# Expert weights in tiles of 16 KB a partition, one-product scatter, tokens gathered from the residual, one softmax

## The chip, the cores and the metric

The kernel runs on one core of a Trainium2 chip. The metric is the device time of one execution in microseconds (us). The profile shows TensorE (PE, with its weight loads as PEld), VectorE (DVE), ScalarE (ACT), GpSimd (POOL) and SyncE (SP), which issues most DMAs. Each engine takes its instructions in order.

## The reference, cut to what matters

One layer over 512 tokens of 1024 features: two token mixers (neighbourhood attention, a bidirectional state-space scan), merged by gates and an output projection, and then experts that each choose 64 tokens:

```
x = x + ga1 * rmsnorm(merge(...) @ w_out, n_post_mix)
h = rmsnorm(x, n_pre_ffn) * (1 + sc2) + sh2
aff = softmax(h @ w_router)                   # 512 x 16
gate, idx = top_k(aff.T, 64)                  # 16 experts, 64 tokens each
xg = h[idx]                                   # 16 x 64 x 1024
hid = silu(xg @ w_eg) * (xg @ w_eu)           # 1024 -> 2048
yo = (hid @ w_ed) * gate                      # 2048 -> 1024
out = x + ga2 * rmsnorm(zeros.at[idx].add(yo), n_post_ffn)
```

All is float32. The weights of an expert are three matrices of 8.39 MB; the sixteen experts have 402.7 MB, read once.

## The kernel before

The mixers come first: an input projection in pieces of split float32 products, the scan, attention, the gates and the merge of the branches, all led by PE. The merge writes the merged branch `uh2` and `ul2` (a high and a low part, 8 x 128 features by 512 tokens).

The tokens are held in two orders. The grid has 8 rows of 64 columns, and most of the program has the tokens as h, r, c (8 column groups, 8 rows, 8 columns in a group); `perm_hrc` and `split_hrc` turn one into the other. Before the change the merged branch, the residual `x1` and all that follows keep h, r, c, so `x` is loaded and the output written in pieces of 64 partitions, 8 x 8 rows of the tensor.

The out projection (`out_part`, L1009 to L1021) makes 128 tokens by 256 columns from 24 products, two such pieces in one call for the last half. It needs `g1`, a gain row spread over all partitions, and evacuates into `h2` through one of three PSUM buffers. `post(i)` finishes a tile of 128 tokens: the residual, eight transposes, the router's logits, the softmax and its transpose into `affn`. `scaled(i)` makes the experts' input `h2` from `x1`: a POOL product with `a2`, an ACT copy with the norm's factor, a POOL sum with `s2`. Both rows are spread over the partitions by DMAs on POOL's queue. The program mixes these pieces by hand, `post(i - 1)` and `scaled(i - 2)` after `out_part(i)`.

Top-k takes eight rounds of `max` and `match_replace` on 16 partitions. From the mask come the slots (`slot`), and from them for each pair of experts a one-hot `oh`. `gather` multiplies it with `h2` on PE and copies into `xg`; the first expert's gather is cut up between its first products.

The experts' loop reads its weights in tiles of 1 MB, 8 KB in each partition, from a ring of 15 (`W_RING`), with four more tiles the first time (`W_FIRST`, the 0 tiles). `wtile` hands them out; the letter is the pool. Pool b lies where the out projection's operands lie, the 0 tiles where the routing's tiles lie, so their loads wait for those. Gate and up tiles have rows of 8 KB of DRAM, down tiles two rows of 4 KB for each partition. Each expert: the products for gate and up (`pu`), four transposes of the one-hot times affinity (`pg` to `pgT`), SwiGLU, transposes of `hid`, the down products (`pd`), a copy `yo`, and the scatter: eight products by `pgT`, K = 64, each added into `ya` by DVE. The last expert's down matrix is read in two column halves, rows of 1 KB, so that the closing norm's squares start before the end.

SP's queue has the weight loads in program order, and a load whose tile is not free holds all behind it.

## Time and profile before

| | |
|---|---|
| median of 3 runs | 2150.54 us (2147.04 to 2150.69) |
| profiled execution | 2140.64 us, span 2138.8 us |
| PE busy | 1956.6 us, 91% of the span |
| DVE, ACT, POOL busy | 877.0, 617.4, 315.4 us |
| DMA | 549.42 MB, mean 257 GB/s |
| granted TensorE clock | 0.981 |

The span runs from the first to the last instruction; the execution's own time lies 1.84 us above it. Busy shares are means over stages: about the first half is token mixing, the second the experts. [...] Times within the span start at its first instruction.

### The profile page before, as it was taken

How to read it: one execution, taken by the hardware profiler on the slowest of the kernel's cores; microseconds unless marked ns; L12 is line 12 of the kernel's file. 1: busy time of each engine (PE TensorE's matmuls, PEld its weight loads, DVE VectorE, ACT ScalarE, POOL GpSimd, SP SyncE). 2: the span in 40 equal slices, each digit the busy share in tenths (PEclk: the TensorE clock that was granted, in tenths of full speed). 3: DMA queues.
4: the chain of work that ended last, by engine and by line, in shares of the span. 5: the costliest groups of instructions: out<-in, count | busy, mean ns of one | idle time of the engine just before them, and what ended most of it. 6: DMA issues, size and time to landing. Idle time of an engine off the chain costs nothing.

```text
span 2138.8 us, 26149 instructions
## 1 busy us (share of the span) xinstructions
PE 1956.6 (91%) x10331; PEld 1194.0 (56%) x10331; DVE 877.0 (41%) x1590; ACT 617.4 (29%) x1222; POOL 315.4 (15%) x397
## 2 busy tenths in 40 slices
PE   5999999999999999999985999998989989898985
PEld 3778787776777777788884343342423333242322
DVE  6797777747665657833336011101111111011112
ACT  2466556435555544632222110000000000000001
POOL 3042312243333323200013000000000000000001
PEclk8999999999999999999996999999999999999998
DMA  9344334352332335553485899999999999999996
GB/s 245 89 137 136 92 116 133 104 155 92 111 128 86 118 118 160 166 167 104 158 246 209 336 417 416 416 417 417 418 418 418 416 417 416 416 416 418 418 416 200
DMA packets 190810, 549.42 MB, mean 257 GB/s; under 512 B 14328, under 2 KB 108584, under 8 KB 155872
## 3 DMA queue, kind: packets, MB, share of 16 engines
q1 hardware_dynamic: 174648, 490.90, 60.1%
q0 software_dynamic: 15680, 55.81, 8.1%
q8 instruction: 81, 1.33, 0.3%
q10 hardware_dynamic: 360, 1.05, 0.1%
q14 instruction: 41, 0.34, 0.0%
HBM read 530.76 MB, written 16.94 MB: 256 GB/s over the span
## 4 chain that ended last, share of the span: by engine, by line
PE 50%; DMA 26%; DVE 6%; issue 4%; POOL 3%; ACT 2%; SPq 0%; POOLq 0%; DVEq 0%; ACTq 0%
PE pu L1169 12%; DMA wb<-in_w_exp_down 5%; DMA wb<-in_w_exp_up 5%; PE ps_mm L213 4%; PE ps_mm L219 4%; PE ps_mm L214 4%; DMA wa<-in_w_exp_down 3%; PE px L1136 3%; DMA wc<-in_w_exp_up 3%; PE pd L1209 2%; PE px L1218 2%; PE ps_mm L929 2%; PE ps_mm L928 2%; DMA wc<-in_w_exp_down 2%; PE ps_mm L927 2%
## 5 line engine op out<-in xcount | busy, mean ns | idle before, releaser
L213 PE MATMUL ps_mm<-hh,wh 128*128 128x512 f32 (+1 forms) x648 | 264.3, 408 | 7.1 <-DVE sz L914 4.6
L214 PE MATMUL ps_mm<-hl,wh 128*128 128x512 f32 (+1 forms) x648 | 259.7, 401 | 2.6 <-DVE hl L352 2.6
L219 PE MATMUL ps_mm<-hh,wl 128*128 128x512 f32 (+1 forms) x648 | 260.4, 402 | 0.0
L167 DVE TENSOR_TENSOR wl<-raw,wh 128x1024 fp32r<-128x1024 f32 (+2 forms) x109 | 141.8, 1301 | 195.0 <-ACT wh L166 189.9
L1169 PE MATMUL pu<-wb,xg 128*64 128x512 f32 x792 | 179.7, 596 | 9.5 <-DMA wb<-in_w_exp_up 5.7
L1224 DVE TENSOR_TENSOR ya<-ya,px 128x512 f32<-128x512 f32 x112 | 70.7, 683 | 281.1 <-PE px L1218 280.6
L166 ACT CAST wh<-raw 128x1024 fp32r<-128x1024 f32 (+2 forms) x109 | 117.0, 1074 | 183.3 <-PE ps_mm L928 84.8
L213 PEld LDWEIGHTS ps_mm<-hh,wh 128*128 128x128 f32 (+1 forms) x648 | 122.3, 189 | 41.5 <-issue 14.3
L214 PEld LDWEIGHTS ps_mm<-hl,wh 128*128 128x128 f32 (+1 forms) x648 | 122.5, 189 | 20.8 <-DVE hl L352 3.3
L219 PEld LDWEIGHTS ps_mm<-hh,wl 128*128 128x128 f32 (+1 forms) x648 | 122.5, 189 | 15.7 <-issue 0.8
L1189 DVE SCALAR_TENSOR_TENSOR hid<-hid,pu 128x512 f32<-128x512 f32 x32 | 21.9, 687 | 249.4 <-ACT hid L1188 249.4
L1169 PEld LDWEIGHTS pu<-wb,xg 128*64 128x64 f32 x792 | 54.3, 137 | 124.1 <-issue 97.7
L1154 POOL DMA_DIRECT2D g<-gain_scr x1 | 0.6, 574 | 817.7 <-PE pu L1169 817.7
L1178 DVE TENSOR_TENSOR pg<-oh,aff 128x256 f32<-128x256 f32 x32 | 12.2, 421 | 262.3 <-PE px L1181 223.7
L1209 PE MATMUL pd<-wb,hidT 128*64 128x512 f32 x384 | 89.7, 600 | 16.2 <-DMA wb<-in_w_exp_down 15.8
L480 DVE SCALAR_TENSOR_TENSOR cacc<-pad,cwh,cacc 128x772 f32<-128x772 f32 (+1 forms) x96 | 100.3, 1049 | 9.6 <-ACT cacc L478 8.6
L1169 PE MATMUL pu<-raw,xg 128*64 128x512 f32 x408 | 94.5, 597 | 5.8 <-DMA raw<-in_w_exp_gate 3.0
L1169 PE MATMUL pu<-wc,xg 128*64 128x512 f32 x408 | 95.0, 596 | 4.2 <-DMA wc<-in_w_exp_up 2.5
L1169 PE MATMUL pu<-wa,xg 128*64 128x512 f32 x408 | 94.0, 597 | 4.2 <-DMA wa<-in_w_exp_up 2.5
L1218 PE MATMUL px<-yo,pgT 64*128 64x512 f32 x240 | 82.5, 634 | 9.6 <-ACT yo L1214 9.6
L216 PE MATMUL ps_mm<-ch,wh 128*128 128x256 f32 x280 | 82.0, 293 | 4.3 <-ACT rw L683 4.2
L1188 ACT ACTIVATE hid<-pu 128x512 f32<-128x512 f32 x32 | 19.0, 597 | 221.8 <-PE pu L1169 221.8
(816 smaller groups left out, 3478.6 us busy)
## 6 DMA issues: line engine op xcount, KB each, us to landing
wb<-in_w_exp_up SPq DMA_DIRECT2D x50, 1024.0 KB
wb<-in_w_exp_gate SPq DMA_DIRECT2D x49, 1024.0 KB
wb<-in_w_exp_down SPq DMA_DIRECT2D x48, 1024.0 KB
...
```

The lines of the kernel that those rows point to most:

```text
L166: S.copy(wh, v[:, :, c0:c0 + n])
L167: eng.tensor_tensor(wl, v[:, :, c0:c0 + n], wh.bitcast(F32), op=OP.subtract)
L213: PE.matmul(lat, wh[:, k, :m], hh[:, k, :], start=s, stop=False)
L214: PE.matmul(lat, wh[:, k, :m], hl[:, k, :], start=False, stop=False)
L216: PE.matmul(ctxp, wh[:, k, :m], ch[:, k, :], start=s, stop=False)
L219: PE.matmul(lat, wl[:, k, :m], hh[:, k, :], start=False, stop=e)
L480: E.scalar_tensor_tensor(acc[:, :n], pad[:, j:j + n], w(j), acc[:, :n], op0=OP.mult, op1=OP.add)
L1136: PE.matmul(p[:, k * 128:(k + 1) * 128], h2[:, i, (k0 + k) * 128:(k0 + k + 1) * 128], oh[:, i].rearrange("p e s -> p (e s)"), start=(i == ...
L1169: PE.matmul(acc[q * 2 + b][o * 64:(o + 1) * 64, :], xe[:, k, :], w[:, f:f + 512], start=(k == 0), stop=(k == KT - 1))
L1209: PE.matmul(pd[dh * 64:(dh + 1) * 64, :], l, wd[:, q1 * 1024 + dh * 512:q1 * 1024 + (dh + 1) * 512], start=(n == 0), stop=(n == 15))
L1218: PE.matmul(p, pgT[dh * 64:(dh + 1) * 64, i * 128:(i + 1) * 128], yo[dh * 64:(dh + 1) * 64, :], start=True, stop=True)
L1224: V.tensor_tensor(d, d, p, op=OP.add)
```

## The change

- Weights: every tile has 2 MB, 16 KB in each partition, from one contiguous stretch of DRAM (two neighbouring rows of gate or up, four of down). The ring has eight tiles, ten the first time; pool d lies where the out projection's results lay. The order of the hidden features follows (`hid` is transposed with a stride of four). The last expert's down matrix comes in two halves with rows of 2 KB.
- Tokens: `h2`, `a2`, `s2` and `scaled` are gone. `gather` reads `x1` with a stride of two features, the one-hot is first multiplied by the norm's factor (`ohq`), and scale and shift (`modg`, per feature) are applied where the product is evacuated.
- Softmax: `post` becomes `resid`, `turn`, `logits`, `second`, and one `soft` over the four tiles.
- Scatter: the bare one-hot is transposed (`ohT`, by a product with the identity, both halves of the partitions), the affinity of each slot is a product of one column (`gs`); `yo` is scaled by it and split into a high and a low part that stand in the two halves of the partitions, so that one product with K = 128 adds both.
- Row order: the merged branch is written in the natural order, and `x` and the output move in pieces of 128 partitions.
- `g1` moves from SP's queue to POOL's, ahead of `x`.
- The last expert calls a Sqrt early, on one column.

```diff
-W_RING = "aaacccrrrbbbbbb"
-W_FIRST = "aaacccrrrbbb0000bbb"
+W_RING = "acsrbbbd"
+W_FIRST = "acsrbb00bd"
...
+        modg = rc.tile([128, 16], F32, name="modg")
+        for c0, src, off in ((0, mod_d, 1024), (8, gain_d, 1024)):
+            G.dma_start(modg[:, c0:c0 + 8].rearrange("p (k a) -> p k a", a=2),
+                        bass.AP(tensor=src.tensor, offset=src.offset + off, ap=[[2, 128], [256, 4], [1, 2]]))
+        return wr2, sb, modg
...
-            split_act(uh2[:, j, :], ul2[:, j, :], t1)
+
+            S.copy(perm_hrc(uh2[:, j, :]), split_hrc(t1))
+            V.tensor_tensor(perm_hrc(ul2[:, j, :]), split_hrc(t1), perm_hrc(uh2[:, j, :].bitcast(F32)), op=OP.subtract)
...
-    h2 = ab.tile([128, 4, D], F32, name="h2")
+    qv = ab.tile([128, 4], F32, name="qv")
+    rx, es_rx = pool("rx", side="right")
+    hx = rx.tile([128, 4, D], F32, name="hx")
     rt, es_rt = pool("rt", side="right")
     spD1, es_spD1 = pool("spD1", side="right")
     brow = lambda t, off: bass.AP(tensor=t.tensor, offset=t.offset + off, ap=[[0, 128], [1, D]])
     g1 = rt.tile([128, D], F32, name="g1")
-    a2 = rt.tile([128, D], F32, name="a2")
-    s2 = rt.tile([128, D], F32, name="s2")
-    with tc.high_priority(offset=HP_G1):
-        nc.sync.dma_start(g1, brow(gain_d, 0))
+    G.dma_start(g1, brow(gain_d, 0))
     for i in range(4):
-        for q in range(2):
-            XQ.dma_start(x1[q * 64:(q + 1) * 64, i, :], x_src[2 * i + q])
-    G.dma_start(a2, brow(gain_d, 1024))
-    G.dma_start(s2, brow(mod_d, 1024))
+        G.dma_start(x1[:, i, :], a["x"][i * 128:(i + 1) * 128, :])
...
+    def soft():
+
+        shp = [128, 4, NE]
+        lg = rt.tile(shp, F32, name="lg")
+        m, r = rt.tile([128, 4], F32, name="lgm"), rt.tile([128, 4], F32, name="lgr")
+        col = lambda t: t.rearrange("p (i o) -> p i o", o=1).to_broadcast(shp)
+        V.tensor_tensor(lg, pl_, col(qv), op=OP.mult)
+        V.tensor_tensor(lg, lg, sb.rearrange("p (o e) -> p o e", o=1).to_broadcast(shp), op=OP.add)
+        V.tensor_reduce(m, lg, axis=AX.X, op=OP.max)
+        V.tensor_tensor(lg, lg, col(m), op=OP.subtract)
+        S.activation(aff, lg, AF.Exp)
+        V.tensor_reduce(r, aff, axis=AX.X, op=OP.add)
         V.reciprocal(r, r)
-        V.tensor_scalar(aff[:, i, :], aff[:, i, :], r, None, op0=OP.mult)
-        PE.transpose(pa[:, i * 128:(i + 1) * 128], aff[:, i, :], ident)
-        V.tensor_copy(perm_hrc(affn)[:, 2 * i:2 * i + 2], split_hrc(pa)[:, 2 * i:2 * i + 2])
-
-    def scaled(i):
-        G.tensor_tensor(h2[:, i, :], x1[:, i, :], a2, op=OP.mult)
-        S.activation(h2[:, i, :], h2[:, i, :], AF.Copy, scale=stt[:, i, 5:6])
-        G.tensor_tensor(h2[:, i, :], h2[:, i, :], s2, op=OP.add)
...
+    out_part(0, 2, 2)
+    resid(0)
+    out_part(1, 2, 2)
+    turn(0)
+    second(0)
+    resid(1)
+    out_part(2, 2, 2)
+    logits(0)
+    turn(1)
+    second(1)
+    resid(2)
+    out_part(3, 2, 2)
+    logits(1)
+    turn(2)
     with tc.high_priority(offset=HP_POST):
-        post(3)
-    scaled(2)
-    scaled(3)
+        resid(3)
+        turn(3)
+        second(3)
+    second(2)
+    logits(2)
+    logits(3)
+    soft()
...
+    es_raw.close()
+    wpr, es_wpr = pool("wpr")
+    wps, es_wps = pool("wps")
+    wpa, es_wpa = pool("wpa")
+    wpb, es_wpb = pool("wpb", bufs=3)
+    wpc, es_wpc = pool("wpc")
...
+    es_rx.close()
+    wpd, es_wpd = pool("wpd", side="right")
...
-    wp0, es_wp0 = pool("wp0", side="right", bufs=4)
+    wp0, es_wp0 = pool("wp0", side="right", bufs=2)
...
-        return rawtile() if c == "r" else order[c].tile([128, 2048], F32, name="w" + c, tag="w" + c)
+        return order[c].tile([128, 4096], F32, name="w" + c, tag="w" + c)
...
+    def split_yo(pd, gs, w):
+
+        yo = yap.tile([128, 2, w], F32R, name="yo", tag="yo", bufs=B_YO)
+        for dh in range(2):
+            S.activation(yo[hv_[dh], dh], pd[hv_[dh]], AF.Copy, scale=gs[hv_[dh]])
+        for dh in range(2):
+            V.scalar_tensor_tensor(yo[hv_[1 - dh], dh], pd[hv_[dh]], gs[hv_[dh]], yo[hv_[dh], dh].bitcast(F32),
+                                   op0=OP.mult, op1=OP.subtract)
+        return yo
...
-                PE.matmul(p[:, k * 128:(k + 1) * 128], h2[:, i, (k0 + k) * 128:(k0 + k + 1) * 128],
-                          oh[:, i].rearrange("p e s -> p (e s)"), start=(i == 0), stop=(i == 3))
-        S.copy(xg[:, k0:k0 + n, :], p.rearrange("p (k n) -> p k n", k=n))
+                f0 = (k0 + k) // 2 * 256 + (k0 + k) % 2
+                PE.matmul(p[:, k * 128:(k + 1) * 128], x1[:, i, f0:f0 + 255:2],
+                          ohq[:, i].rearrange("p e s -> p (e s)"), start=(i == 0), stop=(i == 3))
+        for k in range(n):
+            pk, sc_, sh_ = p[:, k * 128:(k + 1) * 128], modg[:, 8 + k0 + k:9 + k0 + k], modg[:, k0 + k:k0 + k + 1]
+            if n == 1:
+                V.tensor_scalar(xg[:, k0 + k, :], pk, sc_, sh_, op0=OP.mult, op1=OP.add)
+            else:
+                S.activation(xg[:, k0 + k, :], pk, AF.Identity, scale=sc_, bias=sh_)
...
+            ohq = moe.tile([128, 4, 2, CAP], F32, name="ohq", tag="ohq", bufs=1)
+            with tc.high_priority(offset=HP_OH):
+                V.tensor_tensor(oh.rearrange("p i e s -> p (i e) s"), iota.to_broadcast([128, 8, CAP]),
+                                bass.AP(tensor=sl2.tensor, offset=sl2.offset, ap=[list(x) for x in sl2.ap] + [[0, CAP]]),
+                                op=OP.is_equal)
+                V.tensor_tensor(ohq.rearrange("p i e s -> p i (e s)"), oh.rearrange("p i e s -> p i (e s)"),
+                                qv.rearrange("p (i o) -> p i o", o=1).to_broadcast([128, 4, 2 * CAP]), op=OP.mult)
...
-            wg, wu = wtile(), wtile()
-            nc.sync.dma_start(wg, a["w_exp_gate"][e, k * 128:(k + 1) * 128, :])
-            nc.sync.dma_start(wu, a["w_exp_up"][e, k * 128:(k + 1) * 128, :])
-            for q, w in enumerate((wg, wu)):
+            if k % 2 == 0:
+                wgu = []
+                for src in (a["w_exp_gate"], a["w_exp_up"]):
+                    w = wtile()
+                    nc.sync.dma_start(w, src[e, k * 128:(k + 2) * 128, :].rearrange("(p a) f -> p (a f)", a=2))
+                    wgu.append(w)
...
-        pg = yap.tile([128, 4, 2, CAP], F32, name="pg", tag="pg", bufs=1)
-        for b in range(2):
-            V.tensor_tensor(pg[:, :, b, :], oh[:, :, e % 2, :], aff[:, :, e:e + 1].to_broadcast([128, 4, CAP]), op=OP.mult)
-        p = px()
+        p, pgs = px(), px((128, 1))
         for i in range(4):
-            PE.transpose(p[:, i * 128:(i + 1) * 128], pg[:, i].rearrange("p b s -> p (b s)"), ident)
-        pgT = yap.tile([128, T], F32, name="pgT", tag="pgT", bufs=B_PGT)
-        S.copy(pgT, p)
+            o_ = oh[:, i, e % 2, :]
+            for b in range(2):
+                PE.matmul(p[hv_[b], i * 128:(i + 1) * 128], o_, ident, start=True, stop=True)
+            for b in range(2):
+                PE.matmul(pgs[hv_[b], :], o_, aff[:, i, e:e + 1], start=(i == 0), stop=(i == 3))
+        ohT = yap.tile([128, T], F32R, name="ohT", tag="ohT", bufs=B_PGT)
+        S.copy(ohT, p)
+        gs = yap.tile([128, 1], F32, name="gs", tag="gs", bufs=2)
+        V.tensor_copy(gs, pgs)
...
-                PE.transpose(p[:, q * 128:(q + 1) * 128], hid[:, b, q * 128:(q + 1) * 128], ident)
+                PE.transpose(p[:, q * 128:(q + 1) * 128], hid[:, b, q::4], ident)
...
+            S.activation(fin[:, 2, 0:1], hid[:, 1, 0:1], AF.Sqrt, scale=0.0, bias=epst[:, 0:1])
...
-                for q2 in range(2):
-                    wd = wtile()
-                    f0 = (b * 2 + o) * 512 + q2 * 256
-                    nc.sync.dma_start(wd.rearrange("p (a d) -> p a d", a=2),
-                                      a["w_exp_down"][e, f0:f0 + 256, :].rearrange("(a p) d -> p a d", p=128))
...
+                wd = wtile()
+                f0 = (b * 2 + o) * 512
+                nc.sync.dma_start(wd, a["w_exp_down"][e, f0:f0 + 512, :].rearrange("(p a) d -> p (a d)", a=4))
+                for q in range(4):
+                    l = hidT[:, b, q, o * 64:(o + 1) * 64]
+                    for dh in range(2):
+                        PE.matmul(pd[dh * 64:(dh + 1) * 64, :], l, wd[:, q * 1024 + dh * 512:q * 1024 + (dh + 1) * 512],
+                                  start=(n == 0), stop=(n == 15))
+                    n += 1
+        yo = split_yo(pd, gs, 512)
         for i in range(4):
             for dh in range(2):
                 p = px()
-                PE.matmul(p, pgT[dh * 64:(dh + 1) * 64, i * 128:(i + 1) * 128], yo[dh * 64:(dh + 1) * 64, :],
-                          start=True, stop=True)
+                PE.matmul(p, ohT[:, i * 128:(i + 1) * 128], yo[:, dh], start=True, stop=True)
...
-    o_dst = a["out"].rearrange("(r h c) d -> h r c d", r=8, h=8, c=8)
...
-                nc.sync.dma_start(v[:, :, dh, :], a["w_exp_down"][e, f0 * 128:(f0 + per) * 128, dh * 512 + c0:dh * 512 + c0 + w]
-                                  .rearrange("(a p) d -> p a d", p=128))
...
+            src = a["w_exp_down"][e, f0 // 4 * 512:(f0 // 4 + 1) * 512, :].rearrange("(p a) d -> p a d", a=4)
+            nc.sync.dma_start(v, src[:, f0 % 4:f0 % 4 + 2, cs])
...
+                (nc.sync, nc.scalar)[b].dma_start(a["out"][0:128, sl], ya[:, i, sl])
+        if i:
+            (nc.sync, nc.scalar)[i % 2].dma_start(a["out"][i * 128:(i + 1) * 128, :], ya[:, i, :])
```

On POOL, where the out projection begins and after it (g1, g2, a2 and s2 are the gain and shift rows), the order before is:

```order
L997 DMA x1_9198<-in_x 64x1x1024 x8
L998 DMA a2_9209<-gain_scr_7179 128x1024
L999 DMA s2_9210<-mod_scr_3961 128x1024
L1056 TENSOR_TENSOR h2_9201<-x1_9198,a2_9209 128x1024
L1058 TENSOR_TENSOR h2_9201<-h2_9201,s2_9210 128x1024
```

and after it:

```order
L968 DMA t1_9101<-gate_scr_85 128x512
L1001 DMA g1_9215<-gain_scr_7179 128x1024
L1003 DMA x1_9201<-in_x 128x1024 x4
L1211 DMA g2_13078<-gain_scr_7179 128x1024
L1311 TENSOR_TENSOR ya_10088<-ya_10088,g2_13078 128x512 x8
```

The gain row g1 stands first, x has four loads in place of eight, and all products and sums between the gates and the end are gone.

On ACT, in the second half of the out projection (L1020 and L1024 the squares of a product, L1034 and L1040 those of the residual, L1057 the scaling of h2, L1049 and L1070 the exponential), before:

```order
L1020 ACTIVATE scr2_9231,stt_9222<-ps_mm_9475 128x512
L1034 ACTIVATE scr2_9231,stt_9222<-x1_9198 128x512
L1020 ACTIVATE scr2_9231,stt_9222<-ps_mm_9526 128x512
L1034 ACTIVATE scr2_9231,stt_9222<-x1_9198 128x512
L1039 COPY x1T_9586<-ps_t_9597 128x512
L1057 ACTIVATE h2_9201<-h2_9201,stt_9222 128x1024
L1034 ACTIVATE scr2_9231,stt_9222<-x1_9198 128x512
L1049 ACTIVATE aff_9199,stt_9222<-lg_9620,stt_9222 128x16
L1020 ACTIVATE scr2_9231,stt_9222<-ps_mm_9628 128x512
L1034 ACTIVATE scr2_9231,stt_9222<-x1_9198 128x512
L1039 COPY x1T_9688<-ps_t_9699 128x512
```

and after:

```order
L1049 COPY x1T_9589<-ps_t_9596 128x512
L1040 ACTIVATE scr2_9230,stt_9221<-x1_9201 128x512 x2
L1024 ACTIVATE scr2_9230,stt_9221<-ps_mm_9624 128x512
L1049 COPY x1T_9683<-ps_t_9690 128x512
L1040 ACTIVATE scr2_9230,stt_9221<-x1_9201 128x512 x2
L1024 ACTIVATE scr2_9230,stt_9221<-ps_mm_9718 128x512
L1049 COPY x1T_9777<-ps_t_9784 128x512
L1040 ACTIVATE scr2_9230,stt_9221<-x1_9201 128x512 x2
L1049 COPY x1T_9803<-ps_t_9810 128x512
L1070 ACTIVATE aff_9202<-lg_9850 128x64
```

The scaling copies are gone, the exponential stands once at the end.

On SP's queue, behind the last loads of w_out (wa to ws, w0 and raw are the weight tiles of the pools), before:

```order
L994 DMA g1_9208<-gain_scr_7179 128x1024
L1163 DMA wa_9984<-in_w_exp_gate 128x2048
L1164 DMA wa_9985<-in_w_exp_up 128x2048
L1163 DMA wa_10002<-in_w_exp_gate 128x2048
L1164 DMA wc_10003<-in_w_exp_up 128x2048
L1163 DMA wc_10020<-in_w_exp_gate 128x2048
L1164 DMA wc_10021<-in_w_exp_up 128x2048
L1163 DMA raw_10038<-in_w_exp_gate 128x2048
L1164 DMA raw_10039<-in_w_exp_up 128x2048
L1163 DMA raw_10056<-in_w_exp_gate 128x2048
L1164 DMA wb_10057<-in_w_exp_up 128x2048
```

and after:

```order
L1223 DMA wa_9968<-in_w_exp_gate 128x4096
L1223 DMA wc_9970<-in_w_exp_up 128x4096
L1223 DMA ws_10000<-in_w_exp_gate 128x4096
L1223 DMA wr_10002<-in_w_exp_up 128x4096
L1223 DMA wb_10032<-in_w_exp_gate 128x4096
L1223 DMA wb_10034<-in_w_exp_up 128x4096
L1268 DMA wb_10132<-in_w_exp_down 128x4096
L1268 DMA wd_10142<-in_w_exp_down 128x4096
L1223 DMA w0_10064<-in_w_exp_gate 128x4096
L1223 DMA w0_10066<-in_w_exp_up 128x4096
L1268 DMA wa_10152<-in_w_exp_down 128x4096
L1268 DMA wc_10162<-in_w_exp_down 128x4096
```

Four tiles of 2 MB stand ahead of the first wb in place of nine tiles of 1 MB, and the first load is no longer that of g1.

## Rows read from the trace of the kernel before

**Rows 1.** Page, part 2, slices of the span: granted clock; GB/s.

```profile
PEclk8999999999999999999996999999999999999998
...
GB/s 245 89 137 136 92 116 133 104 155 92 111 128 86 118 118 160 166 167 104 158 246 209 336 417 416 416 417 417 418 418 418 416 417 416 416 416 418 418 416 200
```

**Rows 2.** Windows: us; busy us of PE, PEld, DVE, ACT, POOL; clock; DMA share; GB/s.

```profile
1120.00:1130.00 10.00, 2.24 (x11) 2.24 (x12) 1.76 (x3) 2.53 (x6) 6.98 (x3) 0.51 0.06 24
...
1160.00:1170.00 10.00, 3.56 (x27) 3.48 (x28) 6.47 (x15) 0.27 (x1) 0.00 (x0) 0.50 0.59 246
```

**Rows 3.** Timeline of POOL and of ACT, 1070 to 1128: start, length, engine, line; [idle].

```profile
1074.74 4.44 POOL L997 DMA_DIRECT2D x<-in_x  x8 [29.88 <-PE ps_mm L929]
...
1121.74 2.33 POOL L1056 TENSOR_TENSOR h<-x,a 128x1024 f32<-128x1024 f32 x1 [30.69 <-DMA a<-gain_scr]
...
1124.11 1.15 ACT L1057 ACTIVATE h<-h,stt 128x1024 f32<-128x1024 f32 x1 [12.70 <-POOL h L1056]
```

**Rows 4.** DMA issues of the stretch 1070 to 1125: KB, us to landing.

```profile
a<-gain_scr POOLq DMA_DIRECT2D x1, 512.0 KB, 34.4
```

**Rows 5.** Timeline of PE in the out projection.

```profile
1127.76 0.38 PE L1052 MATMUL ps_s<-cn,aff 128*16 128x128 f32 x1 [10.68 <-DVE aff L1051]
...
1134.02 0.28 PE L1017 MATMUL ps_mm<-wl,uh 128*128 128x256 f32 x1
...
1138.22 0.28 PE L1018 MATMUL ps_mm<-wh,ul 128*128 128x256 f32 x1
```

**Rows 6.** Timeline of SP's queue, 1090 to 1216.

```profile
1138.41 0.33 SPq L1164 DMA_DIRECT2D wb<-in_w_exp_up  x1
...
1173.06 5.04 SPq L1204 DMA_DIRECT2D wa<-in_w_exp_down  x3
```

**Rows 7.** Chain that ended last, 1136 to 1180: start, length, what.

```profile
1148.27 1.15 ACT h L1057
...
1149.42 0.30 ACT aff L1049 x2
...
1152.72 0.63 DVE mx L1089
...
1166.38 0.70 DVE oh L1145
...
1167.13 3.78 PE px L1136 x16
```

**Rows 8.** Timeline of SP's queue in the steady experts.

```profile
1384.37 0.33 SPq L1163 DMA_DIRECT2D wb<-in_w_exp_gate  x1
...
1401.76 0.33 SPq L1164 DMA_DIRECT2D wa<-in_w_exp_up  x1
...
1404.25 5.33 SPq L1204 DMA_DIRECT2D wc<-in_w_exp_down  x3
...
1949.21 16.89 SPq L1204 DMA_DIRECT2D wb<-in_w_exp_down  x6
```

**Rows 9.** Chain, last expert's down weights.

```profile
2089.90 5.68 DMA wa<-in_w_exp_down
...
2113.28 1.09 PE pd L1243 x6
```

**Rows 10.** Chain, third expert and the start of the fourth.

```profile
1278.40 7.34 PE px L1136 x64
...
1335.95 8.73 PE pu L1169 x40
```

**Rows 11.** Timeline of DVE, first out products with g1.

```profile
1081.49 0.75 DVE L1021 TENSOR_TENSOR h<-ps_mm,g 128x256 f32<-128x256 f32 x2
```

**Rows 12.** What the tile x answers: shortest, median, longest time to landing.

```profile
DMA to landing us min/median/max: 12.2/26.0/39.9
```

**Rows 13.** Timeline of ACT at the end.

```profile
2119.40 1.28 ACT L1259 ACT_TABLE_LOAD   x1
```

**Rows 14.** Window in the output, columns as in rows 2.

```profile
2132.00:2133.00 1.00, 0.00 (x0) 0.00 (x0) 0.00 (x0) 0.00 (x0) 0.00 (x0) 0.50 0.52 205
```

**Rows 15.** Page, part 5: busy, mean ns of one; idle before.

```profile
L1224 DVE TENSOR_TENSOR ya<-ya,px 128x512 f32<-128x512 f32 x112 | 70.7, 683 | 281.1 <-PE px L1218 280.6
```

More of the change, by code (lines that the diff above doesn't have):

```diff
@@ L34 @@
 HP_POST = 100
+HP_OH = 50
 W_LAST = 256
@@ L944, in emit @@
         if jj == R_AT:
-            wr2, sb = router()
+            wr2, sb, modg = router()
     es_gp.close()
@@ L1038, in post, with logits @@
                 PE.transpose(p[:, k * 128:(k + 1) * 128], x1[:, i, (b * 4 + k) * 128:(b * 4 + k + 1) * 128], ident)
-            (S.copy if b else V.tensor_copy)(xT_[:, b * 4:(b + 1) * 4, :], p.rearrange("p (k n) -> p k n", k=4))
+            (S.copy if b else V.tensor_copy)(xTs[i][:, b * 4:(b + 1) * 4, :], p.rearrange("p (k n) -> p k n", k=4))
+    def logits(i):
         for k in range(KT):
-            PE.matmul(pl_[:, i, :], xT_[:, k, :], wr2[:, k, :], start=(k == 0), stop=(k == KT - 1))
-        V.tensor_reduce(b2, stt[:, i, 7:10], axis=AX.X, op=OP.add)
@@ L1053, in post, with second @@
-        V.tensor_copy(perm_hrc(affn)[:, 2 * i:2 * i + 2], split_hrc(pa)[:, 2 * i:2 * i + 2])
-    def scaled(i):
-        G.tensor_tensor(h2[:, i, :], x1[:, i, :], a2, op=OP.mult)
-        S.activation(h2[:, i, :], h2[:, i, :], AF.Copy, scale=stt[:, i, 5:6])
-        G.tensor_tensor(h2[:, i, :], h2[:, i, :], s2, op=OP.add)
+            PE.matmul(pl_[:, i, :], xTs[i][:, k, :], wr2[:, k, :], start=(k == 0), stop=(k == KT - 1))
+    def second(i):
+        V.tensor_reduce(stt[:, i, 12:13], stt[:, i, 7:10], axis=AX.X, op=OP.add)
+        rsq1(qv[:, i:i + 1], stt[:, i, 12:13], rt)
@@ new lines, in soft @@
+    def soft():
[9 more added lines that the diff above has]
+        V.tensor_reduce(r, aff, axis=AX.X, op=OP.add)
+        V.reciprocal(r, r)
+        V.tensor_tensor(aff, aff, col(r), op=OP.mult)
+        for i in range(4):
+            PE.transpose(pa[:, i * 128:(i + 1) * 128], aff[:, i, :], ident)
+        V.tensor_copy(affn, pa)
@@ L1200, in emit @@
             for o in range(2):
-                for q2 in range(2):
-                    wd = wtile()
-                    f0 = (b * 2 + o) * 512 + q2 * 256
-                    nc.sync.dma_start(wd.rearrange("p (a d) -> p a d", a=2),
-                                      a["w_exp_down"][e, f0:f0 + 256, :].rearrange("(a p) d -> p a d", p=128))
-                    for q1 in range(2):
-                        l = hidT[:, b, q2 * 2 + q1, o * 64:(o + 1) * 64]
-                        for dh in range(2):
-                            PE.matmul(pd[dh * 64:(dh + 1) * 64, :], l,
-                                      wd[:, q1 * 1024 + dh * 512:q1 * 1024 + (dh + 1) * 512],
-                                      start=(n == 0), stop=(n == 15))
-                        n += 1
-        yo = yap.tile([128, 512], F32, name="yo", tag="yo", bufs=B_YO)
-        S.copy(yo, pd)
+                wd = wtile()
[8 more added lines that the diff above has]
+        yo = split_yo(pd, gs, 512)
         for i in range(4):
@@ L1250, in emit @@
                 p = pu() if n and dh else px()
-                PE.matmul(p[:, :w], pgT[dh * 64:(dh + 1) * 64, ts_], yo[dh * 64:(dh + 1) * 64, :], start=True, stop=True)
-                V.tensor_tensor(d[:, dh, :], d[:, dh, :], p[:, :w], op=OP.add)
-            fs = yap.tile([128, 2, w], F32, name="fs", tag="hid", bufs=1)
+                PE.matmul(p[:, :w], ohT[:, ts_], yo[:, dh], start=True, stop=True)
+                V.tensor_tensor(d[:, dh * w:(dh + 1) * w], d[:, dh * w:(dh + 1) * w], p[:, :w], op=OP.add)
+            fs = yap.tile([128, 2 * w], F32, name="fs", tag="hid", bufs=1)
             S.activation(fs, d, AF.Square, accum_out=fin[:, n, i:i + 1])
-            G.tensor_tensor(d, d, halves(g2, c0, w), op=OP.mult)
-        c0 += w
+            G.tensor_tensor(d, d, g2[:, cs], op=OP.mult)
     q = fin[:, 2, :]
```

77 lines of the change are left out of this document (27 added, 50 removed).

## The prediction

> **What bounds the kernel now.** I read the DMA's rate first, over the 40 slices of the span, since the kernel ends with sixteen experts whose weights are 16 x 25.17 = 402.7 MB. From the 24th slice to the last but one it stands at 416 to 418 GB/s [rows 1]: from about 1230 us on, the stream of weights sets the pace. Before that PE is busy in nine tenths of nearly every slice, and of that part the change touches only the token order in which the merged branch is written.
>
> Second, the 10-us windows between the two regimes: the rate falls to 24 GB/s and, once risen, again to 246 [rows 2]. Bytes not moved there are paid at the end. Who holds them back is in the timelines. POOL waits 30.69 us for the broadcast of a2, ACT, in order, 12.70 us for POOL's product, with squares and the router's exponential queued behind [rows 3]; a2 landed 34.4 us after its issue [rows 4]. PE waits 10.68 us for the affinities in the midst of the out projection, whose last matmul ends at 1138.50 [rows 5]. Only then may the weights go on (the wb tiles lie where its operands were): SP issues the next at 1138.41 [rows 6], with nine tiles of 1.05 MB (9.4 MB) fetched so far.
>
> Third, the chain through the routing: the first top-8 starts at 1152.72, and just ahead of it stands ACT's scaling copy (1148.27), which POOL held up, with the last tile's exponential behind it; the gather starts at 1167.13 [rows 7]. The first tile of the ring comes free at 1173.06 [rows 6].
>
> Fourth, the steady experts. From 1384.37 to 1401.76 SP issues seven gate/up tiles (rows of 8 KB), 2.484 us each, 422 GB/s; from 1404.25 to 1949.21 lie nine experts, 60.55 us each, 416 GB/s [rows 8]. So eight down tiles (rows of 4 KB) take 60.55 - 16 x 2.484 = 20.80 us, 2.600 each, 403 GB/s. The last expert's down matrix, 8.39 MB in rows of 1 KB, comes between 2089.90 and 2113.28 [rows 9], 23.4 us, 359 GB/s. On PE an expert with a gather takes 57.55 us from its first gather matmul to the next expert's first product (1278.40 to 1335.95 [rows 10]); one without lacks the gather's 7.34; the mean is 53.9, under the DMA's 60.55.
>
> **The sum.** I count along SP's queue, from the profiled execution (2140.64 us, span 2138.8); the median of the runs is 1.0046 times that. Before: start 1138.4; 393.2 MB left at 416.9 GB/s, 943.2 us; last landing 2113.3. So 2113.3 - 1138.4 - 943.2 = 31.7 us are holes and slower rows, and after it comes a tail of 25.5.
>
> Start. POOL's products, their ACT copy and both broadcasts go, and with them PE's 10.68 us. About 2.3 more go because two tiles' transposes and logits, not three with two transposes of affinities, stand ahead of the last product. The products stay, 48 in each part at 0.12 us (35 of them from 1134.02 to 1138.22 [rows 5]). Against that stands a new wait: g1 goes from SP's queue, ahead of the weights, to POOL's, ahead of x. DVE's first product with g1 is at 1081.49, and behind it in its order stands the split of the next w_out piece [rows 11]. POOL can issue at 1074.74 [rows 3]. A 256-KB piece of x lands 12.2 us after its issue at best and 39.9 at worst [rows 12], beside the weights; g1, first in the queue, at 12.2 comes at 1087. PE's fourth part, for which the first of three PSUM buffers must be free, would start at about 1086, so I charge 1.5 us. Bounds: 0 and, landing like a2 after 34.4 us, 23. x is then due at 1098 to 1125, about when each tile is added up. So 1138.4 becomes 1127.0, -11.4.
>
> Routing. Softmax of four tiles becomes one piece, and the last exponential waits for POOL no longer. I take 13 us for the 14.2 between the last product and the top-k, bounds 11 and 16; from there to the gather 14.4 becomes 15.1, for a product by q of the one-hot's own shape, 0.70 [rows 7]. Gather at 1127.2 + 13 + 15.1 = 1155.3. It reads x1 with a stride of two; its 64 instructions take 7.34 us now [rows 10]. I take no change; the other bound is double, and would bring PE's mean to 57.6.
>
> Bytes. Four tiles of 2.10 MB are there before the start, so 394.3 MB are left, now in rows of 16 KB. On each of 16 engines a row costs 310.5 ns at 8 KB (2.484 x 16 / 128), 162.5 at 4 KB, 45.7 at 1 KB. From 4 and 1 KB the fixed part is 6.8 ns, from 8 and 4 KB 14.5; with either, carried on from 8 KB, 16 KB take 614 or 607 ns, 427 or 432 GB/s. I take 427, the smaller fixed part, since the larger rests on a difference. Then 394.3 / 0.427 = 923.4, -19.8. Bounds: at 418, the page's best slice, 943.3, nothing gained; at 432 912.7, -30.5. [...]
>
> Holes, 31.7 before. Now 2 to start the stream; 8 where the eight-tile ring is full, after three wb tiles (15 us) and until the routing frees wd and w0 and the first products a 2-MB tile; 10 where the w0 tiles are not used again and no tile is free until the first expert's down products; 2 for the last down matrix in rows of 2 KB (6.8 + 2 x 38.9 = 84.6 ns a row, 21.7 us where 427 GB/s would need 19.7); 5 for other traffic. Together 27, -4.7; coarser tiles come free later, so the other end is +10.
>
> Last landing: 1127.0 + 923.4 + 27 = 2077.4.
>
> Tail, 25.5 before. An ACT_TABLE_LOAD of 1.28 us goes [rows 13]. The output, in pieces of 64 partitions as 8 x 8 rows, moves at 205 GB/s with a DMA share of 0.52 [rows 14]; now it has 128 partitions. 2.1 MB take 10.2 us at 205 and 5.1 at 410; the last piece is twice as large, and yo's split adds two instructions of some 0.4. I take -6 for the output and -7.0 in all, bounds 0 and -8. [...]
>
> Covered. In an expert the scatter's 16 instructions become eight of other type, but eight DVE additions of 683 ns [rows 15] still follow, 5.5 us through three buffers; the yo split adds about 1.4 us (two ACT and two DVE instructions for one ACT copy); four transposes of the weighted one-hot become 32 instructions in two sorts, which I put at 2.4 us between 0.6 (the transposes now) and 3.7 (at the gather's 0.115). PE's mean comes to 54 to 55, the DMA's to 25.17 / 0.427 = 58.9: covered by 4 us. Uncovered, each us costs 16.
>
> Sum: -11.4 - 19.8 - 4.7 - 7.0 = -42.9. Span 2095.9, execution 2097.7, times 1.0046 = **2107 us**.
>
> **Rivals.** First, the rate does not rise: 418 to 422 GB/s, bytes 943.3 to 934.4, time 2127 to 2118. For it: sixteen slices between 416 and 418 look like a ceiling. Against it: rows of 1, 4 and 8 KB differ as a fixed cost per row would have it.
>
> Second, PE takes the DMA's place: strided reads of x1 and hid, the one-hot matmuls and the yo chain bring its mean to 60. Then 1155.3 + 16 x 60 + 18.5 = 2133.8, time 2145. It decides from 58.9 on, and needs the worst end of nearly every bound above.
>
> Third, on the other side: rows of 16 KB are fetched slower than those of 8. Below 408 GB/s (966 us for the bytes) all gain is gone; at 390 they take 1011, and the time is 2195. For it: no row of that size is in this trace, nor one DMA of 2 MB. Against it: each step from 1 to 8 KB gained.
>
> [...]
>
> Fifth, g1 lands as a2 did: 21.5 us more of the start, 2129.
>
> **Chances.** Forecast 0.60, rivals in order 0.17, 0.08, 0.07, 0.03, 0.05. A measurement can tell 0.2% here, 4.3 us. Forecast, first and fifth are faster (0.82); the second lies at the border: 0.03 faster, 0.03 same, 0.02 slower; of the rest 0.01 is same. Faster 0.85, same 0.04, slower 0.11. The range runs from 2086 (432 GB/s -10.7, no wait for g1 -1.5, routing -2, output -1, and 6 less of the holes) to 2145, which takes in the first, second and fifth. The forecast's own is 2090 to 2120.
>
> **What would show it.** Slices of 425 to 430 GB/s; 58 to 60 us an expert on SP; the out projection over at 1127, the gather at 1155; weights done at 2077; the output at a DMA share near 1. It is wrong if the slices stay at 417, if DVE waits for g1 beyond 1090, or if PE goes through the experts without a wait for weights.

## The result, and the profile after

The changed kernel takes 2114.0 us (median of 4 runs, 2113.6 to 2116.6), the kernel before 2149.0 beside it (4 runs): a ratio of 0.984, interval 0.982 to 0.986. It is faster, as forecast, and 7 us above the 2107 that was named. The profiled run took 2113.9 us with a span of 2111.8.

The page's rate of the DMA over the slices of the changed kernel, to be held against [rows 1]:

```profile
GB/s 242 95 133 140 81 119 145 105 142 93 112 117 100 113 106 155 150 175 132 112 249 208 310 393 423 428 428 427 428 427 427 428 428 427 428 426 428 427 428 252
```

From the 26th slice to the last but one it is 426 to 428 in place of 416 to 418. The forecast had 427. So the weights pay what was hoped; the rest of the account is found at both ends of their stream.

At its beginning, SP's queue (start, length, line, what):

```profile
1082.51 0.34 SPq L1223 DMA_DIRECT2D wa<-in_w_exp_gate  x1
...
1139.10 0.33 SPq L1223 DMA_DIRECT2D wb<-in_w_exp_gate  x1
...
1179.28 0.33 SPq L1268 DMA_DIRECT2D wa<-in_w_exp_down  x1
```

The first weight was issued at 1074.90 before and at 1082.51 now, the first wb tile at 1139.10, where [rows 6] has 1138.41 and the forecast 1127.0. Nothing of the earlier start has come. From the first weight to the first wb tile it takes 56.6 us, where it took 63.5 before, but the first weight is 7.6 us later. DVE and PE in between, and the windows (columns as in rows 2):

```profile
1095.33 1.09 DVE L1025 TENSOR_TENSOR hx<-ps_mm,g 128x256 f32<-128x256 f32 x3 [6.61 <-DMA g<-gain_scr]
```

```profile
1095.81 0.58 PE L1020 MATMUL ps_mm<-wh,uh 128*128 128x256 f32 x1 [4.55 <-DVE hx L1025]
```

```profile
1090.00:1095.00 5.00, 1.26 (x11) 1.06 (x9) 0.00 (x0) 0.47 (x2) 0.00 (x0) 0.92 1.04 418
...
1095.00:1100.00 5.00, 4.19 (x19) 4.19 (x20) 1.09 (x3) 0.00 (x0) 0.00 (x0) 0.50 0.99 418
...
1170.00:1180.00 10.00, 10.00 (x50) 5.37 (x51) 1.23 (x3) 0.00 (x0) 0.00 (x0) 0.86 0.03 10
```

DVE waited 6.61 us for g1, PE 4.55 us for DVE's release of a PSUM buffer, and then worked for a few microseconds at a granted clock of 0.50 (a share of full speed). The a2 wait of [rows 3] is gone, and g1 has taken part of its place. The third window is the hole with the ring full: 10 GB/s.

At its end, the chain that ended last (start, length, what), and the windows from the last weights to the output:

```profile
2070.09 3.68 PE pu L1229 x16
...
2075.29 7.08 PE pd L1300 x64
...
2087.99 6.20 PE pd L1300 x54
...
2094.21 0.47 ACT yo L1169
```

```profile
2088.00:2090.00 2.00, 2.00 (x20) 1.35 (x22) 0.66 (x2) 0.96 (x4) 2.00 (x2) 1.00 0.50 185
...
2090.00:2092.00 2.00, 2.00 (x22) 1.35 (x20) 0.00 (x0) 0.00 (x0) 1.29 (x2) 1.00 0.05 19
...
2106.00:2108.00 2.00, 0.00 (x0) 0.00 (x0) 1.57 (x2) 0.00 (x0) 0.00 (x0) 0.50 1.00 401
```

The last weights land at about 2090, but PE goes on with down products until 2094.19; before, it had 1.09 us left after the last landing [rows 9]. The output then moves at 401 GB/s with a DMA share of 1.00 in its best window, where [rows 14] has 205 and 0.52. From the reciprocal of the closing norm to the end it is 10.9 us (2100.93 to 2111.8), against 17.8 before (2121.03 to 2138.8).

### The profile page after: what moved, and what is told of

It is laid out like the page before. It is cut to its first block, busy times and chain, and to the rows that moved or that the text cites. A ratio compares the mean times of both kernels' runs of the same rounds, so it can differ in the third digit from the quotient of the medians.

```text
span 2111.8 us, 26456 instructions
## 1 busy us (share of the span) xinstructions
PE 1950.3 (92%) x10643; PEld 1268.6 (60%) x10643; DVE 899.1 (43%) x1612; ACT 636.6 (30%) x1263; POOL 293.4 (14%) x386
## 4 chain that ended last, share of the span: by engine, by line
PE 64%; DMA 12%; DVE 8%; issue 4%; ACT 3%; POOL 1%; DVEq 0%; POOLq 0%; ACTq 0%; SPq 0%
PE pu L1229 17%; DMA wb<-in_w_exp_down 7%; PE pd L1272 6%; PE ps_mm L214 4%; PE ps_mm L215 4%; PE ps_mm L220 4%; PE px L1184 3%; PE px L1279 2%; PE ps_mm L935 2%; PE ps_mm L934 2%; PE ps_mm L933 2%; DMA wc<-in_w_exp_up 2%; PE ps_y L614 1%; PE ps_t L798 1%; DMA wc<-in_w_exp_down 1%
## 5 line engine op out<-in xcount | busy, mean ns | idle before, releaser
L1229 PE MATMUL pu<-wb,xg 128*64 128x512 f32 x752 | 170.9, 593 | 0.0
L1171 DVE SCALAR_TENSOR_TENSOR yo<-pd,gs,yo 64x512 fp32r<-64x512 f32 (+1 forms) x34 | 24.4, 718 | 281.2 <-ACT yo L1169 280.6
L1229 PEld LDWEIGHTS pu<-wb,xg 128*64 128x64 f32 x752 | 75.5, 137 | 81.4 <-issue 54.3
L1169 ACT ACTIVATE yo<-pd,gs 64x512 fp32r<-64x512 f32 (+1 forms) x34 | 22.3, 657 | 232.7 <-PE pd L1272 208.9
L1272 PE MATMUL pd<-wb,hidT 128*64 128x512 f32 x352 | 79.8, 597 | 12.9 <-DMA wb<-in_w_exp_down 12.9
L1279 PE MATMUL px<-yo,ohT 128*128 128x512 f32 x120 | 57.0, 577 | 35.0 <-DVE yo L1171 34.6
L599 ACT ACTIVATE dd<-dd,lnb 128x128 f32<-128x128 f32 x256 | 79.7, 392 | 10.3 <-POOL dd L595 9.9
L222 PE MATMUL ps_mm<-ch,wl 128*128 128x256 f32 x280 | 81.0, 289 | 0.0
L218 PE MATMUL ps_mm<-cl,wh 128*128 128x256 f32 x280 | 80.7, 288 | 0.0
```

What stands on the lines that cost most here:

```text
L218: PE.matmul(ctxp, wh[:, k, :m], cl[:, k, :], start=False, stop=False)
L222: PE.matmul(ctxp, wl[:, k, :m], ch[:, k, :], start=False, stop=e)
L1229: PE.matmul(acc[q * 2 + b][o * 64:(o + 1) * 64, :], xe[:, k, :], w[:, f:f + 512], start=(k == 0), stop=(k == KT - 1))
L1272: PE.matmul(pd[dh * 64:(dh + 1) * 64, :], l, wd[:, q * 1024 + dh * 512:q * 1024 + (dh + 1) * 512], start=(n == 0), stop=(n == 15))
L1279: PE.matmul(p, ohT[:, i * 128:(i + 1) * 128], yo[:, dh], start=True, stop=True)
```

## Experiments

All are timed beside the kernel before, which came to between 2141.7 and 2153.3 us in 32 timed runs.

**Where the start went.** Two runs undo one small thing each.

```diff
-        modg = rc.tile([128, 16], F32, name="modg")      # in router(), among the gates
-        for c0, src, off in ...: G.dma_start(modg...)
+    modg = ab.tile([128, 16], F32, name="modg")          # behind the loads of x
+    for c0, src, off in ...: G.dma_start(modg...)
```

> The changed kernel with one thing moved: the two small loads of modg stand on POOL's queue behind the loads of x, in place of among the gates. In the changed kernel the merge of the branches ends 8.0 us later than before the change (1082.5 against 1074.5), and POOL waited 5.15 us for the write of the gains before the second modg load, with the loads of the gates behind it. Theory A: that wait and the first modg load hold the gate loads back; the merge ends 5 us earlier and the time falls from 2114.0 to about 2109. Theory B: the 8 us are a matter of other transfers in the early stages, with no part of the change in them; the time stays at 2114 within 1.5.

2109.4 us (2108.3 to 2113.8): theory A in the time, but not by the wait that it names. Two landmarks on SP's queue frame the gates, the last store of the attention and the last store of the gates. Between them lie 173.0 us before (757.55 to 930.53), 178.4 in the changed kernel (760.23 to 938.58) and 172.2 here (761.47 to 933.65). In the six profiles of this study with modg among the gates the stretch takes 176.7 to 178.7 us, in the seven without 172.2 to 173.9. So the place of the two loads costs some 5.4 us. The row that theory A goes by is this one of POOL in the changed kernel:

```profile
917.88 0.78 POOL L877 DMA_DIRECT2D modg<-gain_scr  x1 [5.15 <-DMA gain_scr<-gv]
```

The second load of modg needs the gains that an instruction just before it on the same queue has sent out, and while POOL waits for that write, from 912.7 on, the loads of the gates stand behind it. But the whole loss is there before this wait begins: the third store from the last lies 144.8 us behind the first landmark before (902.32) and 150.2 in the changed kernel (910.38), and from it to the last store it is 28.2 us in both. The loss is in a wait of PE further up, here before and after the change, with the five microseconds that follow in the changed kernel (columns as in rows 2):

```profile
865.06 0.47 PE L213 MATMUL ps_mm<-hh,wh 128*128 128x512 f32 x1 [1.63 <-DVE sz L914]
```

```profile
870.71 0.76 PE L214 MATMUL ps_mm<-hh,wh 128*128 128x512 f32 x1 [4.75 <-DVE sz L920]
```

```profile
870.00:875.00 5.00, 4.29 (x10) 3.45 (x11) 4.66 (x7) 2.58 (x4) 2.58 (x4) 0.50 0.38 111
```

PE waits for DVE, and DVE for a load of the tile yt that POOL issues late: at 846.81, behind a wait of 3.44 us, where modg_late has it at 844.91 behind one of 0.79. The wait of PE is 4.75 us in place of 1.63 (1.45 in modg_late), some 3 us more, and the granted clock is 0.50 from 870 to 875, while before the change it stays at 1.00 from 865 to 880: that makes the rest, by an estimate 2.5 us for five at half the clock. Why the first load of modg, 80 us earlier on POOL's queue, moves that load of yt stays open. The 2.7 us that remain of the 8.0 are there at the first landmark, which lies between 757.6 and 762.4 in these profiles, with or without the change: that much is chance.

```diff
-    G.dma_start(g1, brow(gain_d, 0))
+    with tc.high_priority(offset=HP_G1):
+        nc.sync.dma_start(g1, brow(gain_d, 0))
```

> The changed kernel with g1 back on SP's queue, ahead of the weights. In the changed kernel g1 lands 12.45 us after its issue, DVE waits 6.61 us for it and PE stands 4.55 us in the window 1090 to 1100. Theory A: on SP's queue g1 lands within 7 us, as before the change; PE's hole goes, the weights go on 4.5 us earlier, and as the stream of weights sets the end, the time falls to about 2109.5. Theory B: g1 shares the DMA engines with the same weights on either queue and is as late; the time stays at 2114.

2106.0 us (2104.8 to 2108.0), 8.0 less: theory A, and more than it said. From the first weight to the first wb tile the changed kernel has 56.6 us, this one 49.1 (1082.18 to 1131.26): 7.5 where PE's wait was 4.55. The rest is in the main the clock, which stays at 1.00 here from 1080 to 1120; five microseconds at 0.50, as from 1095 to 1100 in the changed kernel, lose 2.5 by an estimate.

**Does the row set the rate?**

```diff
-                    nc.sync.dma_start(w, v_)                          # one DMA a tile
+                    for c_ in range(0, 4096, 2048):                   # rows_8k; 1024 in rows_4k
+                        nc.sync.dma_start(w[:, c_:c_ + 2048], v_[:, c_:c_ + 2048])
```

> The changed kernel, each 2-MB weight tile but those of the last expert's down matrix loaded by two DMAs of 1 MB with rows of 8 KB (of DRAM and in each partition); same tiles, same layout, same ring. Theory A (a fixed cost per row): the slices of the span fall from 427 or 428 to 422 GB/s, the rate of 8-KB rows before the change; 386 MB then take 11 us longer, time about 2125. Theory B (the gain came from elsewhere, as fewer or larger tiles): 427 stays, 2114. PE stays as it is in both.

> The changed kernel, each 2-MB weight tile but those of the last down matrix loaded by four DMAs of 512 KB, 128 partitions with rows of 4 KB. With rows of 8 KB the slices stood at 421 GB/s and the time at 2124.8, with 16 KB at 427.5 and 2114.0. Theory A (a fixed cost per row): 4-KB rows go at 403 to 406 GB/s, as the down tiles did before the change, 386 MB take 48 to 55 us longer than at 427.5, time 2162 to 2169, slower than before the change. Theory B (down tiles before were slow for their two rows a partition, not for the row's size): 415 or more, 2140 or less.

2124.8 us (2120.8 to 2131.4) and 2146.6 (2141.7 to 2150.4). The first is theory A; the second lies between its theories, nearer to A in the rate. The slices, first of 8-KB and then of 4-KB rows:

```profile
GB/s 242 94 137 140 89 109 142 105 160 77 114 114 97 112 109 164 137 178 149 105 234 266 279 422 421 421 421 421 421 421 421 421 421 421 421 421 421 421 421 264
```

```profile
GB/s 249 83 138 136 91 116 133 104 154 91 111 132 82 124 110 157 143 177 116 159 207 265 364 409 409 409 409 409 409 409 409 409 409 409 409 408 408 409 409 241
```

421 and 409 GB/s. On each of 16 engines a row of 4, 8 and 16 KB takes 160.2, 311.3 and 613.2 ns; twice the shorter less the longer gives a fixed 9.1 and 9.4 ns. A fixed cost per row fits all three, between the 6.8 and 14.5 of the prediction. These runs change the size of a DMA along with the row; the run even_odd below, with DMAs of 1 MB and rows of 16 KB, has 427 to 428, where rows_8k with DMAs of 1 MB has 421, so it is the row. The time of rows_8k comes out in part by luck: 421 GB/s cost 13.9 us on 385.9 MB, and the first wb tile is issued 3.9 us sooner (1135.19). The time of rows_4k is 15 us under theory A's, for two reasons: the rate is 409, not 403 to 406 (385.9 MB, 41 us longer: 2155), and the first wb tile is issued at 1130.67, 8.4 us sooner (7.1 of it behind the first weight). Why sooner stands in the landing of g1, on POOL's queue beside the weights (KB, us to landing), with 16-, 8- and 4-KB rows:

```profile
g<-gain_scr POOLq DMA_DIRECT2D x1, 512.0 KB, 12.5
```

```profile
g<-gain_scr POOLq DMA_DIRECT2D x1, 512.0 KB, 10.1
```

```profile
g<-gain_scr POOLq DMA_DIRECT2D x1, 512.0 KB, 7.4
```

The larger the loads beside it, the later g1. What of this is the row and what the size of the DMA is not told apart: in even_odd, with rows of 16 KB in DMAs of 1 MB, g1 lands after 10.9 us, nearer to the 10.1 of rows_8k than to 12.5. Why is not shown.

```diff
-                    nc.sync.dma_start(w, v_)
+                    for c_ in (0, 64):
+                        nc.sync.dma_start(w[c_:c_ + 64], v_[c_:c_ + 64])    # half_dmas
+                    for c_ in (0, 1):
+                        nc.sync.dma_start(w[c_::2], v_[c_::2])              # even_odd, in its place
```

> The changed kernel, each 2-MB weight tile loaded by two DMAs of 1 MB, each of 64 partitions with rows of 16 KB. Theory A (the row's size sets the rate): 427 GB/s and 2114 within 2, as in the changed kernel. Theory B (the size of a DMA does): 422 GB/s, about 2125, as the two DMAs with rows of 8 KB.

> The changed kernel, each 2-MB weight tile loaded by two DMAs of 1 MB, one to the even and one to the odd partitions, rows of 16 KB. The two DMAs of the run half_dmas had the same size and rows and went to the lower and the upper 64 partitions: 220 to 235 GB/s at a DMA share of 1.0, 2755 us. [...] Theory B (64 rows in a DMA, or its 1 MB in large rows, are slow wherever they go): about 220 GB/s and 2750 again.

half_dmas was to be a mere control and took 2755 us, with a wide spread (2648 to 2851), far above all else here; both theories failed. even_odd, with DMAs of the same size and rows, took 2117.0 (2114.2 to 2118.7), where theory B had 2750. One window of each:

```profile
1500.00:1510.00 10.00, 5.35 (x16) 1.77 (x16) 0.00 (x0) 0.00 (x0) 0.00 (x0) 0.83 1.00 220
```

```profile
1500.00:1510.00 10.00, 7.33 (x28) 2.77 (x24) 3.62 (x6) 1.36 (x2) 0.00 (x0) 0.89 1.01 428
```

At the same DMA share, 1.00 and 1.01, 220 GB/s go into 64 neighbouring partitions and 428 into every second one. Size and row are the same, so it is the choice of partitions that makes the difference here. The rate of half_dmas is not the same everywhere: its slices go from 215 to 372 GB/s in the experts, and what lifts some of them stays open.

**What the a2 wait was worth.** On the kernel before:

```diff
+    G.dma_start(a2, brow(gain_d, 1024))
+    G.dma_start(s2, brow(mod_d, 1024))
     for i in range(4):
         for q in range(2):
             XQ.dma_start(x1[q * 64:(q + 1) * 64, i, :], x_src[2 * i + q])
-    G.dma_start(a2, brow(gain_d, 1024))
-    G.dma_start(s2, brow(mod_d, 1024))
```

> The kernel before, with the broadcasts of a2 and s2 issued ahead of the eight loads of x on POOL's queue. Theory A (a2's landing sets PE's 10.68-us wait): a2 lands within 20 us, the wait goes, the weights go on at 1128 in place of 1138, the time falls by 10 to 2138. Theory B (what is behind a2 on the queue takes its place): x lands 10 us later, the residual of the first tiles waits, and of the 10 us less than 4 are left, 2144 or more.

2132.4 us, 18.5 under the 2150.9 beside it (ratio 0.992, 0.990 to 0.993): theory A, by almost twice. a2 lands after 8.9 us, the first wb tile is issued at 1128.36, 10 us sooner than in [rows 6] and 51.6 behind the first weight in place of 63.5, and the span of the profile is 8.7 shorter (2130.1). The other 10 us lie between the profiled run of before and its timed ones, below.

**Pieces of 64 partitions.** Both on the kernel g1_modg_pd further down.

```diff
-        G.dma_start(x1[:, i, :], a["x"][i * 128:(i + 1) * 128, :])
+        for h in range(2):
+            r0 = i * 128 + h * 64
+            G.dma_start(x1[h * 64:(h + 1) * 64, i, :], a["x"][r0:r0 + 64, :])
```

> The kernel of the run g1_modg_pd (2100.5), x loaded by eight DMAs of 64 partitions, one after the other, in place of four of 128. Before the change, beside x in pieces of 64 partitions, the windows 1080 to 1115 had 265 to 288 GB/s at a DMA share of 1.0; after it, 418 at the same share. Theory A (pieces of 64 partitions slow the weights beside them): 260 to 300 GB/s in the windows 1085 to 1105, x and the weights of the first tiles land some 10 us later, and of that at most 3 us reach the end, since the last of them is wanted at 1120: 2100 to 2104. Theory B (it was the 8-KB and 4-KB rows together): 400 and more, 2100.5.

2104.5 us (2099.3 to 2106.8), just above theory A's range. The same window with x in eight pieces and in four:

```profile
1085.00:1090.00 5.00, 5.00 (x44) 5.00 (x44) 0.42 (x1) 1.86 (x3) 0.00 (x0) 1.00 1.04 316
```

```profile
1085.00:1090.00 5.00, 5.00 (x44) 5.00 (x43) 0.43 (x1) 1.81 (x3) 0.00 (x0) 1.00 0.99 419
```

316 and 419 GB/s at a share of 1.04 and 0.99; the windows from 1080 to 1105 have 279 to 316 with eight pieces. So the low rates beside x before the change, 265 to 288, are in the main those of its 64-partition pieces. Whether they cost time is not shown: the profiled run, the quickest of the five, issues the first wb tile at 1126.44, as g1_modg_pd does (1126.47).

```diff
-            (nc.sync, nc.scalar)[i % 2].dma_start(a["out"][i * 128:(i + 1) * 128, :], ya[:, i, :])
+            for h in range(2):
+                r0 = i * 128 + h * 64
+                (nc.sync, nc.scalar)[h].dma_start(a["out"][r0:r0 + 64, :].rearrange("(r c) d -> r c d", r=8),
+                                                  ya[h * 64:(h + 1) * 64, i, :])
```

The first tile's two column halves are split likewise.

> The kernel of the run g1_modg_pd (2100.5) with the output written in pieces of 64 partitions, lower half on SP's queue and upper half on ACT's, each a plain 64 rows (before the change they were 8 x 8 rows with a stride, 205 GB/s at a DMA share of 0.52). Theory A (the outer 8 of the shape halved the engines): plain 64 rows use all, both halves go side by side, share near 1 and 380 to 400 GB/s; 2100.5 within 1. Theory B (64 partitions are what is slow): about 205 GB/s, 2105 to 2107.

2102.3 us (2100.1 to 2105.4), between the two. From the reciprocal to the end it takes 12.6 us (2088.50 to 2101.1), whole tiles 10.8 (2087.62 to 2098.4), 8 x 8 rows 17.8. The window with most traffic:

```profile
2095.00:2097.00 2.00, 0.00 (x0) 0.00 (x0) 0.13 (x1) 0.00 (x0) 0.00 (x0) 0.50 0.99 346
```

The share is near 1, as theory A has it, and the rate below its 380. So of the 7 us that the output gained, 5 came with the rows that lie side by side in the tensor, at a share of 0.99 in place of 0.52, some 2 from whole tiles. The edit still writes the rows as 8 x 8, only without a gap between the groups, so the run does not tell whether the count of 8 or the gap held the share down.

**The scatter.** On g1_modg_pd, `pg`, four transposes, `pgT`, one copy `yo` and eight products of K = 64 are put back.

```diff
-        yo = split_yo(pd, gs, 512)
+        yo = yap.tile([128, 512], F32, name="yo", tag="yo", bufs=B_YO)
+        S.copy(yo, pd)
...
-                PE.matmul(p, ohT[:, i * 128:(i + 1) * 128], yo[:, dh], start=True, stop=True)
+                PE.matmul(p, pgT[dh * 64:(dh + 1) * 64, i * 128:(i + 1) * 128], yo[dh * 64:(dh + 1) * 64, :],
+                          start=True, stop=True)
```

> The kernel of the run g1_modg_pd (2100.5) with the scatter of before: affinity in the one-hot, four transposes, a copy yo, eight products of K = 64. Theory A (covered, as predicted): the experts run at the DMA's pace either way, and only the tail changes, by about 1 us less for yo's split; 2098.5 to 2101.5. In the stretch in which PE runs without waiting for weights, 1220 to 1570, an expert takes PE 56.5 us with the new scatter; theory A expects within 2 us of it with the old. Theory B (the new scatter frees PE, and PE's pace sets the first six experts): 3 us or more slower, 2104 and up.

2098.5 us (2097.0 to 2103.0) against 2100.5 (2099.9 to 2101.0): the same within what the runs tell, theory A in the time. In PE's pace theory A missed by one: by SP's down loads, two experts apart,

```profile
1222.12 0.33 SPq L1265 DMA_DIRECT2D ws<-in_w_exp_down  x1
...
1329.58 0.33 SPq L1265 DMA_DIRECT2D ws<-in_w_exp_down  x1
```

it is 53.7 us an expert, with the new scatter 56.7 (1218.47 to 1331.89). The new scatter costs PE 3 us an expert, which the DMA covers. Where they go is in PE's timeline, old scatter and then the changed kernel, with a window of the latter (columns as in rows 2):

```profile
1260.93 5.53 PE L1277 MATMUL px<-yo,pgT 64*128 64x512 f32 x16 [0.74 <-ACT yo L1273]
```

```profile
1276.06 0.50 PE L1279 MATMUL px<-yo,ohT 128*128 128x512 f32 x1 [2.31 <-DVE yo L1171]
```

```profile
1278.00:1282.00 4.00, 3.77 (x11) 2.47 (x11) 3.72 (x7) 0.00 (x0) 0.00 (x0) 0.57 1.00 426
```

PE waits 2.31 us for the split of yo in place of 0.74 for its copy. In the changed kernel this wait stands 14 times between 1200 and 2080, and in ten of them the granted clock falls to 0.50 there or within 2.5 us. Over the whole span it has a mean of 0.967; in old_scatter it is 0.983.

**Together.** g1 on SP, modg late, and

```diff
-        pd = psx.tile([128, w], F32, name="pd", tag="pd", bufs=1)
+        pd = pu()[:, :w] if n else psx.tile([128, w], F32, name="pd", tag="pd", bufs=1)
```

> The changed kernel with g1 on SP's queue, modg's loads behind those of x, and the second column half of the last expert's down product in a PSUM buffer of its own (now PE waits 2.2 us at 2082 until the split of yo has read the first half). Theory: the gains add: 8.0 for g1 and 4.6 for modg, as measured one by one, and 2 for the PSUM buffer, so 2099.5 (2096 to 2103). Rival: the earlier start meets the full ring, as the routing frees its tiles no earlier by more than that, and less than half of it is kept: 2106.

2100.5 us (2099.9 to 2101.0; ratio 0.977, 0.975 to 0.979): the gains add. Of the PSUM buffer's 2 us only some 0.6 is seen: from the end of the first half's down products to that of the second's it is 11.2 us (2069.63 to 2080.87) in place of 11.8 (2082.37 to 2094.19). This and old_scatter are the fastest of the study, 13 to 16 us under the changed kernel.

## Why the prediction was right, and where it was wrong

The traces differ by 2138.8 - 2111.8 = 27.0 us, the sum had 42.9. Term by term:

| term | forecast | measured |
|---|---|---|
| start of the stream | -11.4 (1127.0) | +0.7 (1139.1) |
| start to gather | 28.3 | 29.6 (to 1168.72) |
| rate | 427 GB/s | 426 to 428 |
| holes and slower rows | 27 | 29 (2090 - 1139.1 - 394.3 / 0.4275) |
| tail | 18.5 | 21.8 (2090 to 2111.8) |

Against the forecast the start is 12.1 us late, the holes take 2 more, the tail 3.3 more, and the rate gives 1 back: 16 us.

**Right.** The cause of the bound, the removal of the a2 wait, and the rate with its reason: the fixed cost per row (9.1 and 9.4 ns by the runs with rows of 4, 8 and 16 KB). The rate is the term that carried most. The output came as reckoned: 6.9 us less, 6 forecast; the 410 GB/s under the 6 were an estimate, twice the 205 of [rows 14], and the best window has 401. The first rival (the rate stays) is excluded by the slices, the third by the same row.

**The step that failed is the start.** The prediction had the first wb tile at 1127.0; it came at 1139.1, 12.1 us later. First, it said that of the early part the change touches only the token order. It left out two loads of 4 KB on POOL's queue. Their place among the gates costs 5.4 us, not by their bytes: a load of yt behind them comes late, PE waits 4.75 us, and the clock falls to 0.50. With 2.7 us of chance this makes the first weight 7.6 us late (g1's issue, 0.4 us, no longer stands ahead of it). Second, g1 was charged 1.5 us and cost 7.5. Its landing was read right (12.2 us taken, 12.5 measured). But PE's fourth part was put 11.7 us behind the first product (1086 against 1074.28), and three parts of 24 products at 0.12 us take 8.6: PE was there after 8.9 and waited 4.55. And the wait was priced by its length, without the granted clock that follows it, 0.50 from 1095 to 1100. Some 1.5 us of the 6 are made good elsewhere in the out projection, which takes 49.1 us without this wait, where the forecast had 50.6. The wait that the fifth rival names thus came, at a third of its price and without its late landing.

**The tail.** The sum took it that the last weight sets the end. With the weights faster, PE paces the last expert: after its last up tile (2070.09) come 3.68 us of products, the hidden layer, 7.08 us of down products, a pause for yo's split, and the second half until 2094.19. This is the second rival in one place, where nothing covers PE any more. Over the rest PE's pace is 56.6 us an expert (six of them, SP's down loads at 1231.30 and 1570.75), 2 above the estimate, against 58.9 for the DMA: covered as forecast, but by 2.3 us and not by 4, since the split of yo brought a wait (2.31 us) and a fall of the clock (0.57 from 1278 to 1282) that the sum did not have.

**The scale.** The forecast from the trace was 2097.7; the profiled run took 2113.9, an error of 16. The factor of 1.0046 added 9.7 and made it 7. That was luck, for the factor was no constant: the profiled run of before, 2140.64, is below all 32 timed ones, while the changed kernel's is at its median. In before_a2_first, with a2 early, four runs lie within 0.8 us (2131.9 to 2132.7), where the kernel before spreads over 11. So the spread, and with it most of the scale, seems to come with the late a2; this is not shown, since its landing in the timed runs is not seen.

**The clock.** The sum had no fall of the granted clock. In the experts all ten falls stand at the waits for yo's split or within 2.5 us of them, and the page's row still has nine tenths there; at both waits of the start the clock was 0.50.
